# Up-projection of a ConvFFN: from the Strassen to the Winograd form of the 7-product scheme, with two early products on raw quarters for ten alternate pairs

## The chip, the cores and the metric

The kernel runs on one core of a Trainium2 chip. The metric is the device time of one execution in microseconds.

## The reference

One layer of a hybrid encoder in float32, for 640 rows (512 prompt frames and 8 streams of 16 frames), 2048 wide: a conditioned RMSNorm, an input projection, gated DeltaNet heads beside sliding-window attention, an output projection with a gated residual, and then the ConvFFN that the change touches:

```
h2 = rms_norm(x, norm2_w) * (1 + scale2) + shift2
u = h2 @ w_up                       # 640 x 2048 by 2048 x 11264 (gate | up)
u_ext = concatenate([ffn_prev, u], axis=1)
u_c = causal_dwconv(u_ext, ffn_conv_w) + ffn_conv_b      # width 3
gt, up = split(u_c, 2, axis=-1)
x = x + gate2 * ((silu(gt) * up) @ w_down)
```

The last two rows of `u_ext` of each stream are an output too.

## The kernel before, in words

Every float32 matrix is split into a high part, rounded to the matmul's float32r type, and the rest as a low part. A product is high x high, high x low and low x high, three matmuls for each 128 x 128 block of weights.

**Up-projection.** The 11264 columns of `w_up` are 88 blocks of 128, interleaved so that blocks 2i and 2i+1 are the gate and the up part of pair i; there are 44 pairs. For each pair the two blocks, the two halves of the 2048 inner columns, and the two halves `s` of the 640 rows (320 columns on chip) make a 2 x 2 by 2 x 2 product, done with 7 block products instead of 8. One block product is 8 inner chunks x 3 matmuls = 24 matmuls of 320 columns, in two weight units `h` of 128 x 512. For each unit: a weight sum `wsum` on VectorE, where the product wants one (5 of 7 products), a cast `whi` on ScalarE, the rest `wlo` on VectorE (`split_next`). `next_unit` keeps up to 4 units split, and weight sums are made 2 units ahead of that.

**Operands.** The activations' quarters are `b11, b12 = x[j]` (row halves 0 and 1 of chunk j) and `b21, b22 = x[j+8]`. `pipe` builds the background steps: multiply by the row's scale (`mul`, VectorE), modulate (`modulated`: ScalarE for the 256 prompt columns, GpSimd for the 64 others, tile `xr`), sum of quarters (`mixed`, on GpSimd, tile `st`), high part (`operand`, ScalarE), low part (`low`, VectorE). High and low parts lie in the tiles of the output projection's input (`mh`, `ml`), in `ex` and in the residual's own tiles (`op`). `feed` takes such steps from the list at a rate of so many per weight unit.

**Order.** Tiles are scheduled by hand: the program order is that of the Python code, and each engine works in order. In `attn_out` the output projection ends with eight blocks done first for row half 0 and then for row half 1, so that the norm and the operands of half 0 are made meanwhile. Then come the early products: products 2 and 4 of pairs 0 to 4, then 5 and 1 of the same pairs, combined on VectorE and GpSimd (`qsq`) and stored in the DRAM tile `pd`. In `ffn` those 5 pairs do only 3 products (6, 7, 3), and load what is stored through SP's queue (`t5`, `e` and a quarter of `fext`). The other 39 pairs do all seven in `ORDER`. The results of the seven products are summed into `fext` (the two blocks' rows before the convolution): on VectorE where PSUM is read, and on GpSimd for `e` and two `fext` quarters. The convolution of a pair (`conv`: `head` on ScalarE, four `tap` on VectorE, `silu`, `gatep`, `gated`, `store`) is cut into steps which run during the next pair, at half-product slots given by `SLOTS`, or `SLOTS2` when the next pair is a short one. The down-projection follows; it already uses the form of the scheme that the change brings to the up-projection.

Of the kernel before, what the change touches and what calls it, by code (L numbers as in the profile page):

```python
# [16 lines left out]
ORDER = (2, 4, 5, 1, 6, 7, 3)  # L17
# [4 lines left out]
NP = 5  # L22
# [7 lines left out]
MIXP = {4: (1, 1), 1: (1, 1), 6: (1, 1), 7: (1, 1), 3: (1, 1)}  # L30
SPOOL = {2: (1, 1), 5: (0, 0), 1: (1, 0), 6: (1, 1), 7: (0, 0)}
OPER = {5: ((0, 0), (0, 1), ALU.add), 2: ((1, 0), (1, 1), ALU.add), 1: ((0, 0), (1, 1), ALU.add), 3: ((0, 0),),
        7: ((0, 1), (1, 1), ALU.subtract), 6: ((1, 0), (0, 0), ALU.subtract), 4: ((1, 1),)}
SLOTS = (1, 3, 2, 4, 4, 6, 7, 8, 10, 10)
SLOTS2 = (9, 10, 9, 10, 10, 10, 11, 11, 11, 11)
# [193 lines left out]
class Kern:  # L229
# [81 lines left out]
    def build_stream(self):  # L311
        d = self.d
        self.units, self.upos, self.spos, self.apos, self.rpos = [], 0, 0, 0, 0
        self.rorder, self.rleft, self.rtile, self.utile, self.ltile = [], {}, {}, {}, {}
        for g in range(4):
            for i in range(3):
                self.add_unit(0, (("e", i, g), d["win"][i, :, g // 2, (g % 2) * 512:(g % 2 + 1) * 512]))
        for i in range(3, 44):
            self.add_block(("in", i), d["win"][i])
        for f in range(KC):  # L320
            self.add_block(("o", f), d["wo"][f])
        for f in range(KC - NF, KC):
            self.add_block(("O", f), d["wo"][f])

        def quarters(tag, i, ps, pool):
            for p in ps:
                for h in range(2):
                    o = OPER[p]
                    src = [((tag + "b" * (p == 3 and i < NP), 2 * i + j, r), d["wup"][2 * i + j][:, r]) for j, r in o[:2]]
                    self.add_unit(h, *src, op=o[2] if len(o) > 2 else None, pool=pool and len(o) > 2 and SPOOL[p][h])  # L330

        for ps in (ORDER[:2], ORDER[2:4]):
            for i in range(NP):
                quarters("v" + str(ps[0]), i, ps, True)
        for i in range(NFF):
            quarters("u", i, ORDER[4:] if i < NP else ORDER, i < NP)
        n = DGRP[0][1]
        for u in range(16 * n // 4):
            self.add_unit(u % 2, (("d", u // 2), d["wdn"][u // 2]))
        for job, p in self.djobs():  # L340
            f = 2 * n + 2 * job
            a = [[(("d", f + j), d["wdn"][f + j], r) for r in range(2)] for j in range(2)]
            t = {k: (("s", f, k), None, 0) for k in (5, 6)}
            src, op = {1: ((a[0][0],), None), 5: ((a[1][0], a[1][1]), ALU.add), 6: ((t.get(5), a[0][0]), ALU.subtract),
                       2: ((a[0][1],), None), 7: ((a[0][0], a[1][0]), ALU.subtract),
                       3: ((a[0][1], t.get(6)), ALU.subtract), 4: ((a[1][1],), None)}[p]
            self.add_unit(tuple(x[2] for x in src), *(x[:2] for x in src), op=op, pool=DPOOL.get(p),
                          keep=t[p][0] if p in t else None)
# [1205 lines left out]
    def phase2(self):  # L1554
# [6 lines left out]
        self.pd = tc.dram_tile([NP, 4, P, HALF], F32, name="pd")  # L1561
# [30 lines left out]
    def attn_out(self, pa, load):  # L1592
# [23 lines left out]
        self.ops, self.ex, self.low, self.temp, self.bg, self.due = {p: [] for p in ORDER}, [], {}, {}, [], 0.0  # L1616
# [11 lines left out]
        for part in range(2):  # L1628
            self.rate = RATE[1 + part]
            for n in range(NP):  # L1630
                t = [pa.tile([P, HALF], F32, tag=f"{x}{part}", name=f"q{x}") for x in ("acc", "sq")]
                if part:
                    m2 = pa.tile([P, HALF], F32, tag=("acc0", "sq0")[n % 2], name="qm2")
                    nc.sync.dma_start(out=m2, in_=self.pd[n, 0])
                for k in range(2):
                    ps = self.product(ORDER[2 * part + k])
                    if k == 0:
                        nc.scalar.copy(out=t[0], in_=ps)
                    else:
                        v.tensor_tensor(out=t[1], in0=ps, in1=t[0], op=(ALU.add, ALU.subtract)[part])  # L1640
                        if part:
                            nc.gpsimd.tensor_tensor(out=t[1], in0=t[1], in1=m2, op=ALU.subtract)
                    nc.sync.dma_start(out=self.pd[n, 2 * part + k], in_=t[k])
            if part == 0:
                self.drain("b")
# [13 lines left out]
    def modulated(self, k, s):  # L1659
# [8 lines left out]
        nc.gpsimd.tensor_tensor(out=xd, in0=xd, in1=bc(A), op=ALU.mult)  # L1668
        nc.gpsimd.tensor_tensor(out=xd, in0=xd, in1=bc(sh), op=ALU.add)

    def mixed(self, p, j):
        (b11, b12), (b21, b22) = self.x[j], self.x[j + 8]
        if p in (2, 5):
            return
        a, b, op = {4: (b21, b11, ALU.subtract), 1: (b11, b22, ALU.add), 6: (b11, b12, ALU.add),
                    7: (b21, b22, ALU.add), 3: (b12, b22, ALU.subtract)}[p]
        t = self.temp[p, j] = self.stile()
        e = self.nc.gpsimd if MIXP[p][j % 2] else self.nc.vector
        e.tensor_tensor(out=t, in0=a, in1=b, op=op)

    def operand(self, p, j):
# [3 lines left out]
        if p in (2, 5):  # L1685
            src = b11 if p == 2 else b22
        else:
            src = self.temp.pop((p, j))
        if p in (2, 4, 5, 1):
            c = HALF * (p in (5, 1))  # L1690
            hi, lo = (t[:, c:c + HALF] for t in self.mix[j + 8 * (p in (4, 1))])
        else:
# [3 lines left out]
            if p == 6:  # L1696
                self.ex.append(self.ox.tile([P, NT], F32R, tag=f"ex{j}", name=f"ex{j}"))
            lo = old(j + 8 if p == 7 else j, int(p == 3))
            hi = old(j + 8, 1) if p == 3 else self.ex[j][:, HALF * (p == 7):HALF * (p == 7) + HALF]
# [31 lines left out]
    def norm_half(self, pool, s, acc, rB):  # L1731
# [19 lines left out]
        if s == 0:  # L1751
            self.bg += self.pipe([[j, j + 8] for j in r], [[(2, j), (4, j)] for j in r], s, rB)
        else:
            self.bg += self.pipe([[j + 8] for j in r] + [[j] for j in r], [[(p, j)] for p in ORDER[2:] for j in r], s, rB)

    def next_bank(self):
        n = self.nbank % 4
        self.nbank += 1
        if n < 2:
            self.btile = [None, None] if n == 0 else self.btile  # L1760
            self.btile[n] = self.main_ps2(n)[0]
        return self.btile[n % 2][:, n // 2, 0:HALF]
# [20 lines left out]
    def ffn(self, fp):  # L1783
# [18 lines left out]
        def up(i):  # L1802
# [8 lines left out]
            e = hs[i] if i < NP else fp.tile([P, HALF], F32, tag="e", name="e")  # L1811
            for q, pr in enumerate(ORDER):
                if i < NP and q < 4:
                    continue
                ps = self.product(pr, lambda: mid(2 * q, t5))
                if pr == 2:
                    nc.scalar.copy(out=t2, in_=ps)
                elif pr == 4:
                    p4 = ps
                elif pr == 5:  # L1820
                    nc.scalar.copy(out=t5, in_=ps)
                    nc.gpsimd.tensor_tensor(out=e, in0=t2, in1=t5, op=ALU.add)
                elif pr == 1:
                    v.tensor_tensor(out=e, in0=ps, in1=e, op=ALU.subtract)
                    step(7)
                    ext = [prep(i, n) for n in range(2)]
                    add(v, quad(ext[1], 0), qin(p4), qin(t2))
                elif pr == 6:
                    v.tensor_tensor(out=t2, in0=ps, in1=e, op=ALU.add)
                elif pr == 7:  # L1830
                    v.tensor_tensor(out=e, in0=ps, in1=e, op=ALU.add)
                    if i < NP:
                        ext = list(short)
                    add(nc.gpsimd, quad(ext[0], 0), quad(ext[1], 0), qin(e))
                elif pr == 3:
                    add(v, quad(ext[0], 1), qin(ps), qin(t5))
                    add(nc.gpsimd, quad(ext[1], 1), quad(ext[0], 1), qin(t2))
                step(2 * q + 1)
                if i == NFF - 1 and q == 3:
                    self.lanes["c"].add(first_chunks())  # L1840
            conv(i, ext)

        short, hs = [], []

        def load_h():
            hs.append(fp.tile([P, HALF], F32, tag="e", name="e"))
            nc.sync.dma_start(out=hs[-1], in_=self.pd[len(hs) - 1, 3])

        def mid(slot, t5):
            step(slot)  # L1850
            n = self.pair
            if n < NP:
                if slot == 8:
                    nc.sync.dma_start(out=t5, in_=self.pd[n, 2])
                elif slot == 10:
                    short[:] = [prep(n, k) for k in range(2)]
                    for o, x in zip(quad(short[1], 0), qin(self.pd[n, 1])):
                        nc.sync.dma_start(out=o, in_=x)
                elif n < NP - 1:
                    load_h()  # L1860

        load_h()
# [13 lines left out]
        def conv(i, ext):  # L1876
# [38 lines left out]
            self.steps += sorted(zip(SLOTS2 if i + 1 < NP else SLOTS, fns), key=lambda x: x[0])  # L1915
# [289 lines left out]
```

## Time and profile before

| | |
|---|---|
| time, median of 3 runs | 3060.53 us (3060.45 to 3063.92) |
| profiled execution | 3059.98 us, span 3058.2 us |
| mean granted TensorE clock | 0.985 of full |
| TensorE (PE) busy | 2930.0 us, 96% |
| VectorE (DVE) busy | 2292.9 us, 75% |
| ScalarE (ACT) / GpSimd (POOL) busy | 1225.1 us, 40% / 842.0 us, 28% |

The output projection of the attention part ends at about 1342 us of the span, the early products at about 1456 us, the short pairs at about 1527 us, and the up-projection at about 2497 us. All instructions are recorded under one helper line (L91), so groups are told apart by tile names; the profile leaves out digits in names, so that `mm` and `mmd` are the two PSUM pools.

### The profile page before, as it was taken

The numbers are of one execution on the slowest core, as the hardware profiler recorded it, in microseconds if no ns is written. First come the engines' busy times: TensorE is split into PE (matmuls) and PEld (weight loads), VectorE is DVE, ScalarE is ACT, GpSimd is POOL, SyncE is SP. The second block draws the span as 40 slices with busy tenths as digits, with TensorE's granted clock in tenths as the row PEclk, the third lists the DMA queues.
The fourth block names the chain that finished last, engine by engine and source line by source line (L and its number), as shares of the span: only waits on it lengthen the run. The fifth ranks groups of instructions, "written<-read, shape, count | busy, mean of one in ns | idle before, by whom it ended". The sixth has DMA issues, their size and how long they took to land.

```text
span 3058.2 us, 53007 instructions
## 1 busy us (share of the span) xinstructions
PE 2930.0 (96%) x19649; PEld 2761.8 (90%) x19649; DVE 2292.9 (75%) x4419; ACT 1225.1 (40%) x2255; POOL 842.0 (28%) x1283
## 2 busy tenths in 40 slices
PE   5999999999999999987799999999999999999999
PEld 2688889998999987886799999999999999999998
DVE  4333446778887533589799989999899978999998
ACT  2323334333333322354344444444444454444432
POOL 2110012323233321167433333333333311111112
PEclk9999999999999999999999999999999999999999
DMA  8755542222223488745633333333333356666665
GB/s 341 288 177 181 185 130 83 79 77 72 83 90 115 161 300 295 235 141 189 200 99 98 98 101 102 103 98 99 107 104 98 98 180 217 204 226 207 213 221 191
DMA packets 219235, 480.74 MB, mean 157 GB/s; under 512 B 52082, under 2 KB 87184, under 8 KB 218960
## 3 DMA queue, kind: packets, MB, share of 16 engines
q1 hardware_dynamic: 185056, 429.99, 42.1%
q0 software_dynamic: 11152, 36.11, 3.5%
q10 hardware_dynamic: 22768, 11.25, 1.4%
q8 instruction: 155, 2.54, 0.3%
q14 instruction: 104, 0.85, 0.1%
HBM read 407.92 MB, written 71.18 MB: 157 GB/s over the span
## 4 chain that ended last, share of the span: by engine, by line
PE 75%; DVE 13%; DMA 5%; issue 4%; POOL 2%; ACT 1%; SPq 0%; DVEq 0%; ACTq 0%; POOLq 0%
PE mm L91 44%; PE mmd L91 20%; DVE wlo L91 4%; PE ada_ps L91 3%; DVE y L91 2%; PE inv_ps L91 2%; DVE wsum L91 1%; DVE dop L91 1%; DMA y<-yd 1%; DMA araw<-in_adaw 1%; PE pos L91 1%; DMA fext<-pd 1%; PE pstep L91 1%; PE pk L91 1%; DMA e<-pd 1%
## 5 line engine op out<-in xcount | busy, mean ns | idle before, releaser
L91 DVE TENSOR_TENSOR wlo<-raw,whi 128x512 fp32r<-128x512 f32 x584 | 445.1, 767 | 306.5 <-ACT whi L91 279.4
L91 ACT CAST whi<-raw 128x512 fp32r<-128x512 f32 x584 | 358.6, 619 | 498.0 <-PE mm L91 366.4
L91 ACT CAST whi<-wsum 128x512 fp32r<-128x512 f32 x600 | 367.2, 619 | 420.2 <-PE mmd L91 157.2
L91 DVE TENSOR_TENSOR wlo<-wsum,whi 128x512 fp32r<-128x512 f32 x600 | 423.2, 706 | 18.5 <-ACT whi L91 15.8
L91 DVE TENSOR_TENSOR wsum<-raw 128x512 f32<-128x512 f32 x455 | 344.9, 758 | 79.2 <-DMA raw<-in_wup 75.2
L91 PE MATMUL mm<-mh,wlo 128*128 128x320 f32 x1280 | 373.8, 312 | 10.1 <-DVE wlo L91 10.0
L91 PE MATMUL mm<-mh,whi 128*128 128x320 f32 x1280 | 373.3, 312 | 8.8 <-DVE qsq L91 6.5
L91 PE MATMUL mm<-ml,whi 128*128 128x320 f32 x1280 | 372.5, 311 | 0.0
L91 PE MATMUL mm<-hh,wlo 128*128 128x320 f32 x1376 | 331.4, 322 | 5.9 <-DVE wlo L91 5.9
L91 PE MATMUL mm<-hh,whi 128*128 128x320 f32 x1376 | 328.8, 320 | 4.5 <-ACT hh L91 3.2
L91 PE MATMUL mm<-hl,whi 128*128 128x320 f32 x1376 | 327.6, 320 | 0.0
L91 PE MATMUL mmd<-dop,whi 128*128 128x320 f32 x1280 | 283.8, 310 | 5.0 <-DVE y L91 4.9
L91 PEld LDWEIGHTS mm<-mh,wlo 128*128 128x128 f32 x1280 | 235.0, 189 | 23.9 <-DVE wlo L91 12.1
L91 PEld LDWEIGHTS mm<-mh,whi 128*128 128x128 f32 x1280 | 235.1, 189 | 19.6 <-ACT whi L91 7.2
L91 PEld LDWEIGHTS mm<-hh,whi 128*128 128x128 f32 x1376 | 231.0, 191 | 21.6 <-issue 13.7
L91 PEld LDWEIGHTS mm<-hh,wlo 128*128 128x128 f32 x1376 | 231.3, 191 | 19.8 <-issue 11.6
L91 PEld LDWEIGHTS mm<-hl,whi 128*128 128x128 f32 x1376 | 230.9, 191 | 19.2 <-issue 15.7
L91 PEld LDWEIGHTS mm<-ml,whi 128*128 128x128 f32 x1280 | 235.1, 189 | 6.9 <-issue 6.7
L91 PE MATMUL mmd<-mh,wlo 128*128 128x320 f32 x768 | 234.5, 312 | 6.1 <-DVE wlo L91 6.1
L91 PE MATMUL mmd<-mh,whi 128*128 128x320 f32 x768 | 234.6, 312 | 0.8 <-ACT qacc L91 0.8
L91 PE MATMUL mmd<-ml,whi 128*128 128x320 f32 x768 | 234.1, 312 | 0.4 <-DVE ml L91 0.4
L91 PEld LDWEIGHTS mmd<-dop,whi 128*128 128x128 f32 x1280 | 213.5, 188 | 7.7 <-ACT whi L91 4.8
(418 smaller groups left out, 6399.2 us busy)
## 6 DMA issues: line engine op xcount, KB each, us to landing
raw<-in_wup SPq DMA_DIRECT2D x206, 512.0 KB, 3.7
araw<-in_adaw SPq DMA_DIRECT2D x256, 256.0 KB, 5.1
raw<-in_wdn SPq DMA_DIRECT2D x88, 512.0 KB, 4.9
raw<-in_win SPq DMA_DIRECT2D x82, 512.0 KB, 3.6
araw<-in_adaw SPq DMA_DIRECT2D x64, 512.0 KB, 6.5
yd<-y SPq DMA_DIRECT2D x80, 320.0 KB, 5.0
y<-yd SPq DMA_DIRECT2D x80, 320.0 KB, 6.2
raw<-in_wo SPq DMA_DIRECT2D x48, 512.0 KB, 5.5
```

The source lines that it names most:

```text
L91: return f(*args, **kw)
```

## The change

The up-projection goes to the Winograd form, which has 4 weight sums and 4 operand sums. Weight sums per pair: product 5 uses a21+a22, product 6 that sum less a11, product 3 a12 less the sum of 6, product 7 a11-a21; products 1, 4 and 2 use raw quarters (`sum_unit`, shared now with the down-projection). A pair has 8 weight sums in place of 10. Operand sums: b12-b11, b22 less that, b22-b12 and b21 less the sum of the second, all on VectorE; products 1, 2 and 3 use raw quarters. Products 6, 3 and 7 accumulate in PSUM on the banks of 1, 5 and 4. Ten pairs (0, 2, ... 18) have products 1 and 2 done early, both in one bank, so that P1 and P1+P2 are copied to `pd`; such a pair then does five products. Their loads from `pd` are issued on GpSimd's queue. The sums of a pair are all on VectorE, and so are the 64-column operations of `modulated`.

```diff
-ORDER = (2, 4, 5, 1, 6, 7, 3)
+UPORD = (1, 5, 6, 4, 3, 7, 2)
-NP = 5
+NP = 10
+SHORT = {2 * k: k for k in range(NP)}
-SLOTS2 = (9, 10, 9, 10, 10, 10, 11, 11, 11, 11)
+SLOTS2 = (4, 6, 5, 7, 7, 8, 9, 10, 11, 11)
...
+        for i, p in self.first_jobs():
+            for h in range(2):
+                product("v", 2 * i, p, h)
+        for i in range(NFF):
+            for p in UPORD[1:6] if i in SHORT else UPORD:
                 for h in range(2):
+                    product("u", i, p, h)
...
+    def sum_unit(self, key, a, p, h, pool=False):
+        t = {k: (key + (k,), None, 0) for k in (5, 6)}
+        a = [[x + (i,) for x, i in zip(row, h)] for row in a]
+        src, op = {1: ((a[0][0],), None), 5: ((a[1][0], a[1][1]), ALU.add), 6: ((t[5], a[0][0]), ALU.subtract),
+                   2: ((a[0][1],), None), 7: ((a[0][0], a[1][0]), ALU.subtract),
+                   3: ((a[0][1], t[6]), ALU.subtract), 4: ((a[1][1],), None)}[p]
...
+    def first_jobs(self):
+        return [x[1:] for x in sorted((2 * i + 3 * (p - 1), i, p) for i in range(NP) for p in (1, 2))]
...
-        for part in range(2):
-            self.rate = RATE[1 + part]
-            for n in range(NP):
...
+        self.rate, banks = RATE[1], {}
+        for k, (n, p) in enumerate(self.first_jobs()):
+            if p == 1:
+                banks[n] = self.next_bank()
+            ps = self.product(p, None, 2, banks[n], p == 1)
+            t = pa.tile([P, HALF], F32, tag=("acc0", "sq0")[k % 2], name="part")
+            nc.scalar.copy(out=t, in_=ps)
+            nc.sync.dma_start(out=self.pd[n, p - 1], in_=t)
+        self.drain("b")
...
-        nc.gpsimd.tensor_tensor(out=xd, in0=xd, in1=bc(A), op=ALU.mult)
-        nc.gpsimd.tensor_tensor(out=xd, in0=xd, in1=bc(sh), op=ALU.add)
+        nc.vector.tensor_tensor(out=xd, in0=xd, in1=bc(A), op=ALU.mult)
+        nc.vector.tensor_tensor(out=xd, in0=xd, in1=bc(sh), op=ALU.add)
...
+        if p in (5, 7, 4):
+            a, b = {5: (b12, b11), 7: (b22, b12), 4: (b21, b11)}[p]
+            t = self.temp[p, j] = self.stile()
+            v.tensor_tensor(out=t, in0=a, in1=b, op=ALU.subtract)
+            if p == 5:
+                v.tensor_tensor(out=b11, in0=b22, in1=t, op=ALU.subtract)
...
+            self.bg += self.pipe([[j, j + 8] for j in r], [[(1, j), (2, j)] for j in r], s, rB)
...
+            self.bg += self.pipe([[j + 8] for j in r] + [[j] for j in r], [[(p, j)] for p in (3, 5, 7, 6, 4) for j in r], s, rB)
...
+            if short:
+                nc.gpsimd.dma_start(out=t2, in_=self.pd[SHORT[i], 0])
+            a, b, c = (self.main_ps2(self.nbank + k)[0] for k in range(3))
+            self.nbank += 3
+            bank = {1: a[:, 0], 6: a[:, 0], 5: b[:, 0], 3: b[:, 0], 2: b[:, 1], 4: c[:, 0], 7: c[:, 0]}
+            u2 = t2 if short else e
...
+                if pr == 1:
                     nc.scalar.copy(out=t2, in_=ps)
                 elif pr == 5:
                     nc.scalar.copy(out=t5, in_=ps)
+                elif pr == 6 and short:
+                    v.tensor_tensor(out=t2, in0=ps, in1=t2, op=ALU.add)
+                elif pr == 6:
+                    nc.scalar.copy(out=e, in_=ps)
+                elif pr == 4:
+                    v.tensor_tensor(out=t5, in0=t5, in1=ps, op=ALU.subtract)
+                elif pr == 3:
+                    step(9)
                     ext = [prep(i, n) for n in range(2)]
+                    add(v, quad(ext[0], 1), qin(ps), qin(u2))
+                    if short:
+                        for o, x in zip(quad(ext[0], 0), qin(self.pd[SHORT[i], 1])):
+                            nc.gpsimd.dma_start(out=o, in_=x)
                 elif pr == 7:
+                    add(v, quad(ext[1], 0), qin(ps), qin(u2))
+                    add(v, quad(ext[1], 1), quad(ext[1], 0), qin(t5))
+                elif pr == 2:
+                    add(v, quad(ext[0], 0), qin(ps), qin(t2))
```

## Rows read from the trace of the kernel before

**Rows 1.** The page: span, busy time, and VectorE in 40 slices.

```profile
span 3058.2 us, 53007 instructions
...
PE 2930.0 (96%) x19649; PEld 2761.8 (90%) x19649; DVE 2292.9 (75%) x4419; ACT 1225.1 (40%) x2255; POOL 842.0 (28%) x1283
...
DVE  4333446778887533589799989999899978999998
```

**Rows 2.** Busy time by stage: stretch, length, engines, clock, DMA share, GB/s.

```profile
1310.00:1341.65 31.65, 25.82 (x169) 24.73 (x167) 28.72 (x43) 17.73 (x39) 23.00 (x34) 0.99 0.38 121
1341.65:1526.97 185.32, 145.51 (x864) 136.54 (x863) 157.32 (x223) 79.20 (x151) 111.31 (x149) 0.92 0.58 187
1526.97:1545.30 18.33, 18.12 (x122) 17.85 (x123) 18.19 (x30) 9.02 (x17) 8.00 (x13) 1.00 0.27 84
1545.30:2497.00 951.70, 951.70 (x6491) 951.70 (x6491) 859.78 (x1428) 442.23 (x735) 317.60 (x521) 1.00 0.32 103
```

The engines stand in the order PE, PEld, DVE, ACT, POOL.

**Rows 3.** The chain of waits in order of time: start, us, what.

```profile
1312.97 1.14 POOL xr L91 x2
...
1384.04 1.09 DVE ml L91
...
1478.20 4.73 DMA fext<-pd
...
1484.69 4.63 DMA e<-pd
...
1494.05 5.04 DMA fext<-pd
...
1545.29 3.52 PE mmd L91 x24
```

**Rows 4.** Timeline of PE: first early product, first product of pair 5.

```profile
1341.65 0.47 PE L91 MATMUL mmd<-mh,whi 128*128 128x320 f32 x1
...
1526.97 0.39 PE L91 MATMUL mm<-mh,whi 128*128 128x320 f32 x1 [0.29 <-DVE e L91]
```

**Rows 5.** Groups of VectorE by shape, 1650 to 2350 us (full pairs).

```profile
L91 DVE TENSOR_TENSOR wsum<-raw 128x512 f32<-128x512 f32 x286 | 215.0, 752 | 58.9 <-DMA raw<-in_wup 55.9
L91 DVE TENSOR_TENSOR wlo<-wsum,whi 128x512 fp32r<-128x512 f32 x284 | 193.8, 682 | 9.0 <-ACT whi L91 7.8
...
L91 DVE SCALAR_TENSOR_TENSOR ftm<-fext,fcw,ftm 128x656 f32<-128x656 f32 x113 | 99.3, 899 | 0.0
...
L91 DVE TENSOR_TENSOR e<-mm,e 128x320 f32<-128x320 f32 x28 | 13.4, 477 | 0.0
...
L91 DVE TENSOR_TENSOR fext<-mm,t 128x256 f32<-128x256 f32 x29 | 12.0, 413 | 0.0
...
L91 DVE TENSOR_TENSOR fext<-mm,t 128x64 f32<-128x64 f32 x29 | 6.1, 211 | 0.0
```

**Rows 6.** Groups of VectorE and of GpSimd by shape, 1290 to 1460 us.

```profile
L91 DVE TENSOR_TENSOR wlo<-wsum,whi 128x512 fp32r<-128x512 f32 x34 | 35.8, 1054 | 3.6 <-ACT whi L91 2.8 <-POOL xr L91 0.7
...
L91 POOL TENSOR_TENSOR st<-xr,xr 128x320 f32<-128x320 f32 x40 | 47.0, 1191 | 0.0
...
L91 POOL TENSOR_TENSOR xr<-xr,A 128x64 f32<-128x64 f32 x32 | 17.6, 551 | 10.5 <-DVE xr L91 10.3
```

**Rows 7.** Timeline of VectorE at the end of the output projection.

```profile
1335.06 4.07 DVE L91 TENSOR_TENSOR acc<-acc,sq 128x320 f32<-128x320 f32 x1 [1.03 <-ACT sq L91]
1339.05 0.68 DVE L91 TENSOR_TENSOR wlo<-raw,whi 128x512 fp32r<-128x512 f32 x1
1339.66 0.68 DVE L91 TENSOR_TENSOR wlo<-wsum,whi 128x512 fp32r<-128x512 f32 x1
1340.26 0.48 DVE L91 TENSOR_TENSOR ml<-xr,mh 128x320 fp32r<-128x320 f32 x1
1340.66 0.48 DVE L91 TENSOR_TENSOR ml<-st,mh 128x320 fp32r<-128x320 f32 x1
```

**Rows 8.** Tile `xd`: its stores on GpSimd's queue, 1250 to 1345 us.

```profile
DMA to landing us min/median/max: 2.1/2.2/3.9
```

More of the change, by code (lines that the diff above doesn't have):

```diff
@@ L323, in build_stream, with product @@
             self.add_block(("O", f), d["wo"][f])
-        def quarters(tag, i, ps, pool):
-            for p in ps:
-                for h in range(2):
[L328 to L336, printed above, removed]
+        def product(tag, i, p, h):
+            a = [[((tag, 2 * i + j, r), d["wup"][2 * i + j][:, r]) for r in range(2)] for j in range(2)]
+            self.sum_unit(("s", tag, i, h), a, p, (h, h))
+        for i, p in self.first_jobs():
[3 more added lines that the diff above has]
+            for p in UPORD[1:6] if i in SHORT else UPORD:
+                for h in range(2):
+                    product("u", i, p, h)
         n = DGRP[0][1]
@@ L341, in build_stream @@
             f = 2 * n + 2 * job
[L342 to L348, printed above, removed]
+            a = [[(("d", f + j), d["wdn"][f + j]) for r in range(2)] for j in range(2)]
+            self.sum_unit(("s", "d", job), a, p, (0, 1), DPOOL.get(p))
+    def sum_unit(self, key, a, p, h, pool=False):
[4 more added lines that the diff above has]
+                   3: ((a[0][1], t[6]), ALU.subtract), 4: ((a[1][1],), None)}[p]
+        self.add_unit(tuple(x[2] for x in src), *(x[:2] for x in src), op=op, pool=pool,
+                      keep=t[p][0] if p in t else None)
+    def first_jobs(self):
+        return [x[1:] for x in sorted((2 * i + 3 * (p - 1), i, p) for i in range(NP) for p in (1, 2))]
     def djobs(self):
@@ L1615, in attn_out @@
                 done(f, i, ps[:, i, 0:HALF])
-        self.ops, self.ex, self.low, self.temp, self.bg, self.due = {p: [] for p in ORDER}, [], {}, {}, [], 0.0
+        self.ops, self.ex, self.low, self.temp, self.bg, self.due = {p: [] for p in UPORD}, [], {}, {}, [], 0.0
         for i in range(2):
@@ L1627, in attn_out @@
         self.drain("w")
-        for part in range(2):
-            self.rate = RATE[1 + part]
-            for n in range(NP):
[L1631 to L1645, printed above, removed]
+        self.rate, banks = RATE[1], {}
[7 more added lines that the diff above has]
+        self.drain("b")
         self.feed(99)
@@ L1667, in modulated @@
         xd = x[:, 256:HALF].rearrange("p (b t) -> p b t", t=TS)
-        nc.gpsimd.tensor_tensor(out=xd, in0=xd, in1=bc(A), op=ALU.mult)
-        nc.gpsimd.tensor_tensor(out=xd, in0=xd, in1=bc(sh), op=ALU.add)
+        nc.vector.tensor_tensor(out=xd, in0=xd, in1=bc(A), op=ALU.mult)
+        nc.vector.tensor_tensor(out=xd, in0=xd, in1=bc(sh), op=ALU.add)
     def mixed(self, p, j):
+        v = self.nc.vector
         (b11, b12), (b21, b22) = self.x[j], self.x[j + 8]
[L1673 to L1679, printed above, removed]
+        if p in (5, 7, 4):
[4 more added lines that the diff above has]
+                v.tensor_tensor(out=b11, in0=b22, in1=t, op=ALU.subtract)
     def operand(self, p, j):
@@ L1684, in operand @@
         (b11, b12), (b21, b22) = self.x[j], self.x[j + 8]
[L1685 to L1691, printed above, removed]
+        src = self.temp.pop((p, j)) if p in (5, 7, 4) else {1: b11, 2: b21, 3: b22, 6: b11}[p]
+        if p in (1, 2, 3, 5):
+            c = HALF * (p in (3, 5))
+            hi, lo = (t[:, c:c + HALF] for t in self.mix[j + 8 * (p in (2, 3))])
         else:
@@ L1751, in norm_half @@
         if s == 0:
[L1752 removed]
+            self.bg += self.pipe([[j, j + 8] for j in r], [[(1, j), (2, j)] for j in r], s, rB)
         else:
[L1754 removed]
+            self.bg += self.pipe([[j + 8] for j in r] + [[j] for j in r], [[(p, j)] for p in (3, 5, 7, 6, 4) for j in r], s, rB)
     def next_bank(self):
[L1757 removed]
         self.nbank += 1
[L1759 to L1762, printed above, removed]
+        return self.main_ps2(self.nbank)[0][:, 0, 0:HALF]
     def product(self, p, step=None, nh=2, ps=None, first=True):
@@ L1810, in up @@
             t2, t5 = (fp.tile([P, HALF], F32, tag=n, name=n) for n in ("t2", "t5"))
-            e = hs[i] if i < NP else fp.tile([P, HALF], F32, tag="e", name="e")
-            for q, pr in enumerate(ORDER):
-                if i < NP and q < 4:
+            e = None if i in SHORT else fp.tile([P, HALF], F32, tag="e", name="e")
+            short = i in SHORT
+            if short:
+                nc.gpsimd.dma_start(out=t2, in_=self.pd[SHORT[i], 0])
+            a, b, c = (self.main_ps2(self.nbank + k)[0] for k in range(3))
@@ L1814, in up @@
+            self.nbank += 3
+            bank = {1: a[:, 0], 6: a[:, 0], 5: b[:, 0], 3: b[:, 0], 2: b[:, 1], 4: c[:, 0], 7: c[:, 0]}
+            u2 = t2 if short else e
+            ext = []
+            for q, pr in enumerate(UPORD):
+                if short and pr in (1, 2):
                     continue
-                ps = self.product(pr, lambda: mid(2 * q, t5))
-                if pr == 2:
+                ps = self.product(pr, lambda: step(2 * q), 2, bank[pr][:, 0:HALF],
+                                  pr in (1, 5, 4, 2) or short and pr == 6)
+                if pr == 1:
@@ L1817, in up @@
                     nc.scalar.copy(out=t2, in_=ps)
-                elif pr == 4:
-                    p4 = ps
                 elif pr == 5:
                     nc.scalar.copy(out=t5, in_=ps)
[L1822 to L1825, printed above, removed]
+                elif pr == 6 and short:
[6 more added lines that the diff above has]
+                    step(9)
@@ L1826, in up @@
                     ext = [prep(i, n) for n in range(2)]
-                    add(v, quad(ext[1], 0), qin(p4), qin(t2))
-                elif pr == 6:
-                    v.tensor_tensor(out=t2, in0=ps, in1=e, op=ALU.add)
+                    add(v, quad(ext[0], 1), qin(ps), qin(u2))
+                    if short:
+                        for o, x in zip(quad(ext[0], 0), qin(self.pd[SHORT[i], 1])):
+                            nc.gpsimd.dma_start(out=o, in_=x)
                 elif pr == 7:
[L1831 to L1837, printed above, removed]
+                    add(v, quad(ext[1], 0), qin(ps), qin(u2))
@@ L1838, in up @@
+                    add(v, quad(ext[1], 1), quad(ext[1], 0), qin(t5))
+                elif pr == 2:
+                    add(v, quad(ext[0], 0), qin(ps), qin(t2))
                 step(2 * q + 1)
-                if i == NFF - 1 and q == 3:
+                if i == NFF - 1 and q == 2:
                     self.lanes["c"].add(first_chunks())
             conv(i, ext)
[L1843 to L1862, printed above, removed]
@@ L1914, in conv @@
                    lambda: tap(0, 2), silu, gatep, gated, store)
-            self.steps += sorted(zip(SLOTS2 if i + 1 < NP else SLOTS, fns), key=lambda x: x[0])
+            self.steps += sorted(zip(SLOTS2 if i + 1 in SHORT else SLOTS, fns), key=lambda x: x[0])
         ap = self.ap
```

12 lines of the change are left out of this document (4 added, 8 removed).

## Prediction

> **What bounds the kernel now.** I read the page first. TensorE (PE) is busy 96% of the span and VectorE (DVE) 75%, but the slices of DVE show that it is no average: it is at 9 or more tenths in the second half [rows 1]. So the question is which stage leaves PE waiting, and I cut the second half with the busy time by stage. The pairs 5 to 43, from 1545.3 to 2497 us, have PE busy for all of 951.7 us and at full clock, with DVE at 859.8 [rows 2]: there PE is the bound, a product of 24 matmuls takes 3.52 us [rows 3], a full pair 7 x 3.52 = 24.64, and no saving on DVE or GpSimd (POOL) can show. The change does not alter the number of products: 20 are taken early before and after (four for 5 pairs, now two for 10), and the rest later. What can change is PE's lost time, and it lies in one place.
>
> That place has three parts. (a) The end of the output projection, 1310 to 1341.65 us: 169 matmuls, which at 3.52/24 = 0.1467 us are 24.8 us, in 31.65 us: 6.9 lost [rows 2, 3]. (b) and (c) From the first early product to the first product of pair 5 [rows 4]: 185.32 us for 20 early products and 5 short pairs of 3, 35 x 3.52 = 123.2: 62.1 lost, of which 39.8 are idle PE (185.32 - 145.51) and most of the rest goes with a granted clock of 0.92, that is, some of it at the lower level of 1.2 GHz [rows 2]. (d) To 1545.3, five products in 18.33: 0.7. Together 69.7 us, and that is nearly all there is to win.
>
> The chain of waits names the causes. At the end of the projection it runs through POOL's small multiplies on the residual (`xr`) and its sums `st`; in the early products through DVE's splits and `ml`; in the short pairs through two loads from `pd` one after the other, `fext<-pd` and then `e<-pd`, of about 5 us each, and comes round every 15.9 us, where three products are 10.56 [rows 3]. The first two causes are one: DVE and POOL hinder each other. Alone, DVE starts a 512-column split 0.60 us after the one before and a 320-column sum after 0.40 [rows 7]; in this stretch the same split averages 1.05, and one 320-column `acc` sum takes 4.07 [rows 6, 7]. POOL's 320-column sums take 1.19 us [rows 6].
>
> **The change, part by part.**
>
> *Output projection and first operands.* The 64 `xr` operations on 64 columns (0.55 us each on POOL [rows 6]) go to DVE, where 64 columns cost 0.21 by the row and 0.14 after pipelining [rows 5]. No operand sum is left in the first half (products 1 and 2 take raw quarters), so POOL keeps one small residual add per block. The background feeds 0.4 steps per weight unit of 1.76 us, one step per 4.4 us. DVE needs per step two multiplies and two low parts (4 x 0.40), four small operations (0.14 to 0.21, 0.8 at most), 2.5 splits (1.5), and its share of residual and `acc` work (two rows of `fext` size and a 0.40 sum per 4 units: about 0.55): 4.45 at the most. It hardly fits. What POOL lost disappears, but DVE is full: of 6.9 us I leave 3 (0 if the small operations pipeline, 7 if nothing is won).
>
> *Early products.* All 20 need only operands 1 and 2, ready from the first half, so PE need not wait for the second norm; it is hidden behind 70.4 us of products. Before, two of four products needed operands of the second half. DVE's work in these 40 units: 40 splits x 0.60 = 24; the second half's 16 multiplies x 0.40 = 6.4; 32 small x 0.14 to 0.21 = 4.5 to 6.7; mixed operands 5 (two sums), 7 and 4, 32 x 0.40 = 12.8; 40 low parts x 0.40 = 16; the short chain of the norm, about 4 (the same as now); first sums 1.8. Sum 70 to 72 us against PE's 70.4. The weight sums of before and the `qsq` sums are gone; products 1 and 2 accumulate in one bank, and each needs only a ScalarE (ACT) copy and a store. So DVE is exactly full, and it is front-loaded: at 1.3 steps per unit the first 16 steps (multiply, two small, low, and from the eleventh on two mixed) put some 28 us on DVE in 12 units of 1.76 = 21.6 us. Up to three split units lie ahead, 5.3 us. I take 7 us lost, 0 if the lead covers it, 18 if the splits stay at 1.05 us [rows 6] for want of the relief.
>
> *Entry into the pairs.* The tiles of this stage hand their space to the tiles of the pairs; the first `t2` load waits for that. It is needed 7 us after the pair begins. 3 us, 0 to 8.
>
> *Short pairs.* Ten of them, at 0, 2, ... 18, with five products (17.6 us), between full pairs (24.64). DVE per full pair is now 859.78/951.7 x 24.64 = 22.26 us [rows 2]. After: two weight sums fewer (0.752 less 0.07 of overlap, 2 x 0.68), two 320-column sums fewer (2 x 0.41) and two two-piece adds more (2 x (0.34 + 0.14)) [rows 5]: 22.26 - 1.36 - 0.82 + 0.96 = 21.04. A short pair has four splits (4 x 0.61) and one two-piece add (0.48) fewer and one 320-column sum more: 18.53, at prices which still hold POOL's hindrance. So a short pair asks 0.9 us more of DVE than PE takes, the full one beside it 3.6 less; the two together 39.6 against 42.24, and the lead in split units lends the difference. DVE's waits for raw weights (58.9 us in 700 [rows 5], about 2 per pair) are of an engine that is ahead. I take 0.3 us per short pair, 3 in all; 0 to 16 (1.6 us each, if nothing is lent and prices are the means of the rows).
>
> *Loads of the early products.* `t2<-pd` and `ext[0]<-pd` go from SP's queue to POOL's. The `t2` load waits until the pair before has added its last product, and is used after product 6, 7.04 us into the pair. Stores from POOL's queue landed in 2.1 to 3.9 us with DVE some 90% busy [rows 2, 8]. Queued behind it on POOL are only `fext` clears and state copies, which are needed ten microseconds later. The `ext[0]` load is issued after product 3 and is first read after product 5 of the next pair, some 10 us on. Nothing, with 3 us of cover. The ten fewer 512-KB weight loads lie beside PE and give nothing.
>
> *New waits in a pair.* Products 6, 3 and 7 accumulate on the banks of 1, 5 and 4, whose readers have at least one product (3.52 us) of time; the one on DVE, `t5 - ps`, is due as soon as product 4 ends, where DVE waits anyway. Nothing. In full pairs POOL's chain of `e` and `fext` sums, up to now hidden behind PE, goes away: nothing either.
>
> *Clock.* The remaining 16 us of stalls will cost some low clock: now 39.8 us idle go with 0.08 x 185 = 15 us of it, so 6; and the small matmuls of the norm stay, 1.5.
>
> **Sum.** Lost after: 3 + 7 + 3 + 3 + 6 + 1.5 = 23.5 us against 69.7: 46 us won. The profiled execution took 3059.98 us, 1.8 over its span and 0.55 under the median: 3059.98 - 46 = 3014, with the median's half microsecond and roundings 3014 still. I forecast 3014 us.
>
> **A rule against it.** Stores that POOL issues land within 3.9 us while DVE runs at 90% [rows 2, 8]. The Trainium skill (SBUF — State Buffer, SBUF: two separate sides) warns that a DMA issued from the GpSimd queue can starve, since the engine is shut out of the port that it shares with VectorE and can't write descriptors, and advises the SP or ACT queue; that would make the loads late. The page ties this to VectorE's two-port modes, which it says two-input sums do not have; no run so far shows such a delay for loads from `pd`. This is rival 2.
>
> **Rivals.**
> 1. *The early stage stays DVE-bound, or the alternation does.* For it: DVE at 100% of PE's time in my own sum. Against: POOL's hindrance goes. With splits at 1.05 us, 11 us more than I took; with 1.6 us per short pair, 13 more: with either 3025 to 3027, with both 3038. Chance 0.22.
> 2. *The loads on POOL's queue become the wait of every short pair*, as `fext<-pd` and `e<-pd` are now. The place is `t2` after product 6. PE stalls when the load lands later than 7.04 + 5.3 (the split units ahead) = 12.3 us into the pair; the change is slower than before when each of the ten loses more than (46 + 6)/10 = 5.2 us, a landing after 17.5 us. At 7 us each the time is 3014 + 70 = 3084. Against: landings of 2.1 to 3.9 us [rows 8]. Chance 0.05.
> 3. *It does not free PE*: the lost time is set by the second norm's chain wherever it stands, and the ten short pairs lose in all what the five did (25 us) and the early products what they did: 3060. Chance 0.02; the chain needs operands that the first 20 products no longer use.
> 4. *All slack is used*: 5 us lost in all, 3059.98 - 64.7 = 2995. Chance 0.05.
> The forecast itself (2997 to 3024): 0.66.
>
> **Numbers.** About 0.2% (6 us) is what a measurement here can tell from no change. Faster: 0.66 + 0.22 + 0.05 = 0.93; same 0.02; slower 0.05. The range 2997 to 3037 holds the forecast's cases and most of rival 1's.
>
> **What would show it.** Right: POOL's `st` and `xr` groups gone, and its busy time in the full pairs down by about half; 20 early products in under 85 us; a pair of short and full in 42.3 us with PE at 100%; full pairs from 20 on unchanged at 24.64; the chain of waits all PE from the first short pair on. Wrong: DVE at 100% with PE below 90% over the early products longer than 85 us; PE waiting for `wlo` in each short pair; DVE waiting for `t2<-pd`; PE waiting for `t5` before product 7.

## The result, and the profile after

The changed kernel takes 3008.94 us (median of 4 runs, 3005.06 to 3011.95) against 3060.49; the ratio is 0.9831, 95% interval 0.9814 to 0.9848. The forecast was 3014 us, in a range of 2997 to 3037. The same kernel run again with the last experiments gave 3009.55.

The page of the kernel after: span, busy time, VectorE (DVE) in 40 slices.

```profile
span 3006.0 us, 52752 instructions
...
PE 2916.6 (97%) x19649; PEld 2748.6 (91%) x19649; DVE 2191.2 (73%) x4535; ACT 1237.7 (41%) x2299; POOL 556.8 (19%) x964
...
DVE  4233345778788442479888888888888869999998
```

Busy time by stage (columns as in [rows 2]): the end of the output projection, the early products in three pieces up to 1414 us, a stretch with short pairs (a full pair between each two), one of full pairs alone; and below, in one line, the whole stage of the twenty early products.

```profile
1310.00:1338.26 28.26, 27.32 (x184) 26.60 (x182) 24.21 (x65) 19.45 (x42) 3.46 (x8) 1.00 0.43 141
1338.26:1360.00 21.74, 21.73 (x154) 20.63 (x153) 16.09 (x47) 12.74 (x28) 0.87 (x2) 1.00 0.58 201
1360.00:1391.00 31.00, 26.50 (x162) 24.92 (x161) 30.31 (x83) 20.75 (x45) 0.00 (x0) 0.94 0.37 128
1391.00:1414.00 23.00, 23.00 (x158) 23.00 (x158) 21.74 (x47) 18.34 (x44) 0.00 (x0) 1.00 0.66 225
...
1420.00:1650.00 230.00, 230.00 (x1570) 230.00 (x1569) 201.29 (x370) 109.37 (x183) 42.32 (x108) 1.00 0.39 127
...
1850.00:2400.00 550.00, 550.00 (x3752) 550.00 (x3752) 454.09 (x826) 261.58 (x449) 89.35 (x190) 1.00 0.31 100
```

```profile
1338.26:1419.70 81.44, 76.92 (x509) 74.25 (x508) 73.84 (x184) 55.16 (x121) 0.87 (x2) 0.98 0.51 175
```

One stall is left, at 1360 to 1391 us, with DVE busy 30.3 of 31 us. From there on the TensorE (PE) is busy to 1650 us without a gap, through more than half of the short pairs, and idle for 0.1 us in the rest of them. The early products and short pairs of before took 185 us for 123 [rows 2, 4]. The chain of waits of the kernel after says the same; a few pieces of it:

```profile
1366.21 0.55 DVE xr L88 x2
1366.93 0.48 DVE ml L88
1367.41 0.60 DVE wlo L88
...
1390.99 7.05 PE mmd L88 x48
1398.05 7.04 PE mm L88 x48
```

**One measure for all kernels.** Single runs of one kernel differ by 5 us and more, partly in stages that no edit touches (PE had 8257 instructions behind it at 1300 us before, 8242 after). So I count PE's instructions from 1300 to 2400 us of the span, where every kernel is somewhere between the output projection and the last full pairs: 1100 us less 3.52/24 = 0.1467 us for each is the time lost there. (The small matmuls of the norm count like the others, and a few records are missing; the changed kernel, run twice, gave 7440 and 7441, and experiments 5 and 8, which cost nothing in this stretch, 7441 each.) Kernel before, then after:

```profile
1300.00:2400.00 1100.00, 1054.15 (x7047) 1043.82 (x7046) 984.59 (x1591) 509.81 (x879) 439.51 (x679) 0.99 0.36 116
```

```profile
1300.00:2400.00 1100.00, 1094.45 (x7440) 1090.79 (x7439) 937.68 (x1788) 548.57 (x967) 176.31 (x404) 1.00 0.36 117
```

1100 - 7047 x 3.52/24 = 66.4 us lost before, 8.8 after: 57.6 us won here. The spans differ by 52.2. The other 5 went outside: by the same count the changed kernel is 2 us behind at 1300 us, and loses 24 us after 2400 us where the kernel before lost 21. Whether the change has a part in that is not shown; experiment 1, in the old scheme, loses 24 there too.

A correction to what stands above: the first short pair before begins at 1444.3 us, where `ex` first feeds PE, not at 1456. So of the 62.1 us, 32 were lost in the early products (102.6 us for 70.4) and 30 in the short pairs (82.7 for 52.8):

```profile
1341.65:1444.28 102.63, 84.29 (x503) 78.70 (x503) 97.21 (x132) 48.84 (x100) 72.59 (x78) 0.92 0.51 169
1444.28:1526.97 82.69, 61.22 (x363) 57.84 (x361) 60.10 (x92) 30.36 (x51) 38.71 (x72) 0.92 0.67 209
```

### The profile page after: what moved, and what is told of

The parts are those of the page before. It is cut to its first block, busy times and chain, and to the rows that moved or that the text cites. A ratio compares the mean times of both kernels' runs of the same rounds, so it can differ in the third digit from the quotient of the medians.

```text
span 3006.0 us, 52752 instructions
## 1 busy us (share of the span) xinstructions
PE 2916.6 (97%) x19649; PEld 2748.6 (91%) x19649; DVE 2191.2 (73%) x4535; ACT 1237.7 (41%) x2299; POOL 556.8 (19%) x964
## 4 chain that ended last, share of the span: by engine, by line
PE 72%; DVE 12%; issue 10%; DMA 3%; POOL 2%; ACT 1%; SPq 0%; ACTq 0%; DVEq 0%; POOLq 0%
PE mm L88 40%; PE mmd L88 22%; DVE wlo L88 3%; PE ada_ps L88 2%; DVE y L88 2%; PE inv_ps L88 2%; DVE wsum L88 1%; DVE dop L88 1%; DMA araw<-in_adaw 1%; POOL xr L88 1%; PE pos L88 1%; PE pstep L88 1%; POOL xd L88 1%; PE pk L88 1%; PE pl L88 0%
## 5 line engine op out<-in xcount | busy, mean ns | idle before, releaser
L88 DVE TENSOR_TENSOR wlo<-raw,whi 128x512 fp32r<-128x512 f32 x672 | 481.2, 721 | 338.2 <-ACT whi L88 310.2
L88 ACT CAST whi<-raw 128x512 fp32r<-128x512 f32 x672 | 413.3, 619 | 500.5 <-PE mm L88 359.9
L88 ACT CAST whi<-wsum 128x512 fp32r<-128x512 f32 x512 | 317.1, 619 | 391.9 <-PE mmd L88 170.5
L88 DVE TENSOR_TENSOR wlo<-wsum,whi 128x512 fp32r<-128x512 f32 x512 | 349.7, 688 | 92.3 <-ACT whi L88 91.2
L88 PE MATMUL mm<-dop,whi 128*128 128x320 f32 x960 | 213.1, 310 | 4.2 <-DVE y L88 3.9
```

Source lines behind the costliest of these rows:

```text
L88: return f(*args, **kw)
```

## The experiments

My theory was that DVE and GpSimd (POOL) hinder each other, that twenty products on raw quarters hide the second half's preparation, and that alternation with fewer loads frees the short pairs. The main rival: the place of the sums does not matter, only the scheme does.

### 1. The sums of the kernel before on VectorE

```diff
-MIXP = {4: (1, 1), 1: (1, 1), 6: (1, 1), 7: (1, 1), 3: (1, 1)}
-SPOOL = {2: (1, 1), 5: (0, 0), 1: (1, 0), 6: (1, 1), 7: (0, 0)}
+MIXP = {4: (0, 0), 1: (0, 0), 6: (0, 0), 7: (0, 0), 3: (0, 0)}
+SPOOL = {2: (0, 0), 5: (0, 0), 1: (0, 0), 6: (0, 0), 7: (0, 0)}
...
-        nc.gpsimd.tensor_tensor(out=xd, in0=xd, in1=bc(A), op=ALU.mult)
-        nc.gpsimd.tensor_tensor(out=xd, in0=xd, in1=bc(sh), op=ALU.add)
+        nc.vector.tensor_tensor(out=xd, in0=xd, in1=bc(A), op=ALU.mult)
+        nc.vector.tensor_tensor(out=xd, in0=xd, in1=bc(sh), op=ALU.add)
...
-                            nc.gpsimd.tensor_tensor(out=t[1], in0=t[1], in1=m2, op=ALU.subtract)
+                            v.tensor_tensor(out=t[1], in0=t[1], in1=m2, op=ALU.subtract)
```

> The kernel before, its scheme and its five short pairs kept, with the operand sums, the early pairs' weight sums, the sums of the early products and the 64-column operations moved from GpSimd to VectorE. My theory (the two engines hinder each other, but the early stage has also too much VectorE work in this scheme): the early products' stage shortens from 114 us to about 96 to 102, which is VectorE's own sum for it, the output projection's end loses 3 us less, the short pairs stay at 15.4 to 15.9 us each because their loads set them: 3040 to 3052 us. Rival (GpSimd carried work off VectorE, which is the bound there): the 114 us of GpSimd work come on top of a full VectorE, 3085 us or more.

Measured: 3046.54 us, ratio 0.9959 (0.9944 to 0.9974); 7154 instructions and 50.7 us lost from 1300 to 2400 us (the stretch of every such count below). The early products, then the short pairs:

```profile
1338.97:1437.00 98.03, 85.17 (x540) 79.97 (x538) 94.16 (x223) 51.47 (x107) 1.24 (x2) 0.97 0.60 196
1437.00:1510.42 73.42, 58.26 (x326) 55.31 (x325) 54.84 (x95) 27.23 (x44) 22.25 (x56) 0.86 0.67 212
```

VectorE's list of the early stage, by shape:

```profile
L91 DVE TENSOR_TENSOR wlo<-wsum,whi 128x512 fp32r<-128x512 f32 x36 | 24.8, 688 | 1.6 <-ACT whi L91 1.6
L91 DVE TENSOR_TENSOR wsum<-raw 128x512 f32<-128x512 f32 x36 | 24.7, 686 | 0.0
L91 DVE TENSOR_TENSOR st<-xr,xr 128x320 f32<-128x320 f32 x32 | 15.6, 487 | 0.0
```

A split takes 0.688 us where it took 1.054 [rows 6], so DVE does POOL's work as well, and the twenty products take a little less time, 98.0 us (before 102.6). The short pairs, which I had expected to stay as they were, lose 20.6 us instead of 30 (the weight sums of their product 6 have moved to DVE too); their chain of waits is still that of the loads:

```profile
1462.34 5.52 DMA fext<-pd
...
1469.58 3.27 DMA e<-pd
...
1494.11 4.98 DMA fext<-pd
```

So the hindrance is real, and ending it by this move is worth some 16 us net, less than a third of the gain: 9 in the short pairs, 5 in the early products, 2 at the end of the projection.

### 2. The changed kernel with operand sums and 64-column operations on GpSimd

```diff
-        nc.vector.tensor_tensor(out=xd, in0=xd, in1=bc(A), op=ALU.mult)
-        nc.vector.tensor_tensor(out=xd, in0=xd, in1=bc(sh), op=ALU.add)
+        nc.gpsimd.tensor_tensor(out=xd, in0=xd, in1=bc(A), op=ALU.mult)
+        nc.gpsimd.tensor_tensor(out=xd, in0=xd, in1=bc(sh), op=ALU.add)
...
     def mixed(self, p, j):
-        v = self.nc.vector
+        v = self.nc.gpsimd
```

> The changed kernel with the operand sums and the 64-column operations back on GpSimd. My theory (hindrance): the splits and low parts of the early products slow down again and the stage of 20 products grows from 76 us by 10 to 25, 3018 to 3035 us. Rival (the gain is in the raw operands of the first 20 products, wherever the sums run, since PE no longer waits for the second half): 3005 to 3013 us, as the changed kernel.

Measured: 3008.15 us (3007.05 to 3012.46); 7416 instructions, 12.3 us lost. My theory fell here: the hindrance comes back in the rows, but not in the time.

```profile
1300.00:2400.00 1100.00, 1092.38 (x7416) 1088.38 (x7416) 933.35 (x1692) 545.84 (x962) 235.66 (x491) 1.00 0.36 116
```

```profile
L88 DVE TENSOR_TENSOR wlo<-raw,whi 128x512 fp32r<-128x512 f32 x34 | 29.6, 872 | 11.4 <-ACT whi L88 11.4
...
L88 DVE TENSOR_TENSOR ml<-st,mh 128x320 fp32r<-128x320 f32 x8 | 8.3, 1039 | 1.3 <-ACT mh L88 1.3
```

Splits are slow again (0.872 us), yet only 3.5 us more are lost than in the changed kernel. What POOL takes off DVE about pays for what it costs, but not evenly: with the 64-column operations alone on POOL 4.1 us are lost (experiment 9), so the operand sums cost 8 us there and the small operations save nearly 5. POOL's operations on `xr` and `st` make 26% of the chain from 1340 to 1420 us, and ScalarE waits 14.5 us for the sums from 1340 to 1400; how much of the loss is that wait, and how much the slow splits, was not separated.

### 3. Consecutive short pairs

```diff
-SHORT = {2 * k: k for k in range(NP)}
+SHORT = {k: k for k in range(NP)}
```

> The changed kernel with pairs 0 to 9 as the short ones in place of 0, 2, ... 18. My theory: VectorE's 18.5 us at the prices of before, or some 17.1 at the clean prices of the changed trace, stand against 17.6 us of PE; with clean prices nothing is lost (3006 to 3012 us), with the others 0.9 us for each of ten (3018 us). Rival (a short pair needs a full one beside it, to hide its loads and the convolution before it): as in the kernel before, 3 to 5 us for each of ten, 3040 to 3060 us.

Measured: 3032.57 us (3027.83 to 3034.43); 7242 instructions, 37.8 us lost, 29 more than alternate. The time lies between the two expectations. The whole stretch, then the timelines of VectorE and of SP's queue in one pair:

```profile
1300.00:2400.00 1100.00, 1075.46 (x7242) 1067.74 (x7241) 913.66 (x1743) 532.69 (x939) 201.28 (x394) 0.99 0.36 114
```

```profile
1481.67 0.68 DVE L88 TENSOR_TENSOR wsum<-raw 128x512 f32<-128x512 f32 x1
1482.28 0.68 DVE L88 TENSOR_TENSOR wlo<-wsum,whi 128x512 fp32r<-128x512 f32 x1
1487.10 0.69 DVE L88 TENSOR_TENSOR wsum<-raw 128x512 f32<-128x512 f32 x1 [4.14 <-DMA raw<-in_wup]
```

```profile
1474.62 2.29 SPq L88 DMA_DIRECT2D md<-ftm  x2
1482.38 1.79 SPq L88 DMA_DIRECT2D raw<-in_wup  x4
```

DVE is not full; it stands 4.1 us a pair (eight times from 1420 to 1590 us) for a weight load issued at 1482.38, the moment that its sum of 1481.67, the last of product 7, has given back a raw tile. Neither of my two mechanisms, but a third.

### 4. Consecutive, with a22 loaded first

```diff
-        src, op = {1: ((a[0][0],), None), 5: ((a[1][0], a[1][1]), ALU.add), 6: ((t[5], a[0][0]), ALU.subtract),
+        src, op = {1: ((a[0][0],), None), 5: ((a[1][1], a[1][0]), ALU.add), 6: ((t[5], a[0][0]), ALU.subtract),
```

> The kernel of the consecutive short pairs, with one more edit: product 5 names its quarters as a22 + a21, so that a22 is loaded before a21. The five raw tiles are a ring; now a21's load takes the tile of the pair's first quarter, which is given back two products earlier. My theory (each short pair waits some 4 us for a weight load that could not be issued before product 7 of the pair before gave a tile back): the wait falls to about that of the next quarter, 1 to 2 us, and 12 to 22 of the 25 us come back: 3010 to 3020 us. Rival (the wait is for the early products' loads or the convolution's tiles on GpSimd's queue): no change, 3027 to 3037 us.

Measured: 3010.50 us (3006.50 to 3011.59); 7443 instructions, 8.4 us lost: all 29 us came back with one swapped pair of names.

```profile
1300.00:2400.00 1100.00, 1093.28 (x7443) 1089.62 (x7442) 939.05 (x1788) 547.56 (x967) 192.44 (x404) 1.00 0.36 117
```

So the order of loads in the ring of raw tiles, and nothing else, made consecutive short pairs dear. That in the alternate order a full pair's product 2 and the next one's product 1 give the loads the time is my reading; no run tests it.

### 5. Loads on SP's queue

```diff
-                nc.gpsimd.dma_start(out=t2, in_=self.pd[SHORT[i], 0])
+                nc.sync.dma_start(out=t2, in_=self.pd[SHORT[i], 0])
...
-                            nc.gpsimd.dma_start(out=o, in_=x)
+                            nc.sync.dma_start(out=o, in_=x)
```

> The changed kernel with the loads of the early products issued on SP's queue in place of GpSimd's. My theory: the load of t2 waits on SP for the last sum of the pair before, and the weight loads queue behind it; up to 2 us per short pair where the weights come late, 3009 to 3030 us. Rival (a load on GpSimd's queue is starved while VectorE works, so SP is the better place): faster than the changed kernel, below 3005 us; but PE is shown busy all through the short pairs there, so there is nothing to win.

Measured: 3001.20 us (3000.22 to 3003.68), below 3005 as the rival has it, but 7441 instructions, one more than the changed kernel: nothing is lost or won in the stage, so the lower time is not the loads' doing there. PE had 8262 instructions behind it at 1300 us, 20 more than in the changed kernel's profile, so some 3 us of the lower total arose ahead of the edit; where the rest of it came from stays open. In the changed kernel the loads on POOL's queue landed in 2.3 to 4.1 us, here on SP's in 2.2 to 6.2:

```profile
DMA to landing us min/median/max: 2.3/2.6/4.1
```

```profile
DMA to landing us min/median/max: 2.2/4.9/6.2
```

### 6. Alternation alone, in the scheme of before

```diff
+SH = {2 * k: k for k in range(NP)}
...
-                if i < NP and q < 4:
+                if i in SH and q < 4:
...
-                elif n < NP - 1:
-                    load_h()
+            if slot == 12 and n + 1 in SH:
+                load_h()
```

The other tests of `i < NP` and the places in `pd` follow in the same way.

> The kernel before with its five short pairs at 0, 2, 4, 6, 8 in place of 0 to 4, all else kept. Rival to be tested: alternation alone frees the short pairs of their loads, and their 30 us of lost time go, 3030 to 3040 us. My theory: a three-product pair has 10.56 us of PE against some 15 us of VectorE work and the same two loads, of which the full pair beside it can lend only part; 5 to 20 us are won, 3040 to 3055 us.

Measured: 3064.83 us (10 runs), ratio 1.0019 (1.0009 to 1.0028); 6992 instructions, 74.5 us lost. Neither expectation: alternation makes the old scheme slower, by 8 us in this count and 6 in the medians. Its chain of waits shows where:

```profile
1527.81 4.57 DMA raw<-in_wup
...
1534.24 1.74 POOL fext L92 x2
1536.00 5.64 DMA e<-pd
```

A weight load stands in the chain at four of the five short pairs, and the load of `e` behind it at three. `e` has one tile: its load starts when POOL's `fext` sums of the full pair have read it, and DVE's sum after product 6 waits for it. So the run tests alternation with this one tile; with more tiles for `e` it was not run.

### 7. Half as many early products

```diff
-NP = 10
+NP = 5
-RATE = (0.4, 1.3, 1.0)
+RATE = (0.4, 2.6, 1.0)
```

> The changed kernel with ten early products for five short pairs (0, 2, ... 8) in place of twenty, and the background steps fed at 2.6 per unit, so that they are again all given out within the stage. My theory: it is the number of early products on raw quarters that hides the second half's preparation: 10 products are 35 us, VectorE's work there is 60 to 65 us, so 20 to 30 us more are lost: 3027 to 3040 us. Rival (short pairs have a cost of their own, so fewer of them are as good): 3003 to 3014 us.

Measured: 3023.43 us (3018.14 to 3029.31); 7309 instructions, 28.0 us lost, 19 more than with ten pairs, all before 1410 us:

```profile
1350.00:1370.00 20.00, 13.99 (x91) 12.95 (x89) 18.78 (x58) 15.06 (x32) 0.00 (x0) 0.98 0.29 101
1370.00:1390.00 20.00, 15.32 (x59) 13.86 (x60) 19.53 (x49) 11.66 (x26) 0.00 (x0) 0.59 0.30 95
1390.00:1410.00 20.00, 15.58 (x79) 13.67 (x79) 20.00 (x44) 11.68 (x27) 8.52 (x9) 0.83 0.24 73
1410.00:1430.00 20.00, 20.00 (x138) 20.00 (x137) 13.99 (x26) 8.92 (x15) 2.54 (x5) 0.99 0.33 114
```

That is some 4 us under what I expected, but on the theory's side: DVE is 97% busy for 60 us, PE has products for 35 of them, and part of the stalled time passes at a granted clock of 0.59. The doubled rate of the steps belongs to the edit; what it costs by itself was not tested.

### 8. Ten weight sums in the full pairs

The two sums of product 7 are computed twice in pairs 20 to 43.

> The changed kernel with the two weight sums of product 7 computed twice in each of the pairs 20 to 43, so that VectorE makes ten weight sums per pair there again. My theory: full pairs are bound by PE, the saving of the 4+4 form is not seen there, and the 24 x 1.2 us of added work disappear under PE: 3004 to 3012 us, pairs at 24.64 us. Rival (VectorE's load counts in the full pairs too): up to 29 us longer, 3015 to 3038 us.

Measured: 3006.23 us; the full pairs:

```profile
1850.00:2400.00 550.00, 550.00 (x3752) 550.00 (x3751) 478.28 (x871) 257.63 (x446) 88.59 (x189) 1.00 0.31 101
```

DVE does 24 us more, PE the same 3752 matmuls: the two weight sums that the scheme saves are worth nothing in a full pair.

### 9. The steps spread, and the 64-column operations alone on GpSimd

```diff
+            self.rate = 0.9 if k < 12 else 1.75
```

> The changed kernel with the background steps of the second half fed at 0.9 per weight unit during the first 12 early products and at 1.75 after, in place of 1.3 throughout. My theory: the one stall that is left (31 us for 162 matmuls, 7 us lost) comes from VectorE's work being bunched where multiplies, modulation and two operand sums of product 5 fall together; spread out, it fits under PE, and 5 to 7 us of it go: 3000 to 3005 us. Rival (the second norm's chain or ScalarE sets the stall): no change, 3005 to 3012 us, with the stall moved.

Measured: 3005.88 us (3003.73 to 3007.01), 7438 instructions, 9.1 us lost. The idle time moved to 1370 to 1430 us (3.6 us of it) and the loss did not shrink; with this spread at least, bunching does not decide. Other spreads were not run.

> The changed kernel with the 64-column operations alone back on GpSimd, the operand sums on VectorE. My theory now (VectorE's own sum in the stage of the early products is as long as PE's, so what is taken off it shortens the stall): VectorE loses 6 us of work in the stage and GpSimd hinders it less than with the sums: 2 to 5 us faster than the changed kernel. Rival (any GpSimd work there costs VectorE as much as it saves): as the changed kernel, within 2 us.

> The changed kernel again, unedited, beside the others on the same chip, to have an interval for the few microseconds that tell its variants apart: 3003 to 3011 us.

Measured: 3004.57 us (3000.02 to 3008.64) with the two operations of `modulated` on GpSimd, 7472 instructions, 4.1 us lost; the changed kernel beside it 3009.55 (3004.21 to 3014.61) and 7441, 8.7 lost. Of the 4.6 us between them 2.5 lie in the stall at 1360 to 1391 us, which has 179 instructions where it had 162:

```profile
1360.00:1391.00 31.00, 27.31 (x179) 26.00 (x178) 30.52 (x65) 21.96 (x50) 6.64 (x14) 1.00 0.45 161
```

```profile
1300.00:2400.00 1100.00, 1096.20 (x7472) 1093.78 (x7470) 936.85 (x1740) 549.68 (x969) 204.52 (x466) 1.00 0.36 118
```

The intervals against the kernel before (0.9811 to 0.9845, and 0.9825 to 0.9864) overlap, so the totals alone don't tell the two apart; the stage does. Of all versions this one loses least in the stage; the lowest median is that of experiment 5 (3001.20), which the stage does not account for.

## Why the prediction was right, point by point

- *The number.* Nearer than the working deserves. In its stage the change won 57.6 us where 46 were forecast: the loss that is left, 8.8 us (12 as the sum counts it: 81.44 - 70.4 for the early products, and 1.3), lies nearer to the 5 of rival 4 than to the forecast's 23.5. Of the 11 or 12 us between, only 5 show in the time, because about as much went ahead of and behind the stage, for which the sum had no term. That part is luck.
- *Where the loss lay.* Right: 57.6 of the 66.4 us between 1300 and 2400 us went, and full pairs kept their 24.64 us; experiment 8 shows that DVE's saving does not count there.
- *Output projection's end.* 3 us forecast; 28.26 - 184 x 0.1467 = 1.3 measured. DVE was not full, as feared, but 86% busy (24.21 of 28.26 us). From 1310 to 1345 us POOL's `xr` operations were 34% of the chain before; the one small residual add per block that is left makes 3% of it.
- *Early products.* 7 us forecast at the front of the stage; (31 - 162 x 0.1467) = 7.2 measured, later than forecast (PE idle from 1370 to 1390 us, 30 us and more into the stage) but among the steps named, with DVE at 98% and its row of multiply, modulation and operand-5 sums in the chain. The sum "70 to 72 us against 70.4" was the right reading (73.84 us measured, in a stage of 81.44): spreading the work gains nothing (9), taking work off DVE gains 4.6 us (9), halving the products costs 19 (7). Bunching, which I gave as the reason for 7 rather than 0, is not borne out.
- *Hindrance of the two engines.* The step that I got wrong in kind. I called it the cause of the first two losses, 39 us; moving the sums off POOL is worth 6 us in those two parts of the old scheme and 9 in the short pairs, where I had not put it (1), and 3.5 in the new one (2). Where the rows showed slow instructions I took their price for the price of the stage.
- *Entry and short pairs.* 3 + 3 us forecast, none measured: PE is busy for all of 1420 to 1650 us. DVE's load over a short and a full pair was 201.29/230 x 42.24 = 37.0 us against the 39.6 of the sum; a weight sum fell from 0.753 to 0.687 us and a split of a raw block from 0.794 to 0.688 (means of 1550 to 2400 us before and 1440 to 1650 us after), which is about 2 of the 2.6 us. That alternation was needed is true with this order of loads, but not for the reason given (DVE's lent time): the raw ring decides (3, 4). What freed the short pairs of their 30 us is only narrowed down: not the order of the pairs (4, 6) and not the queue of the loads (5). The longer pair (17.6 us for 10.56) and the loads' new places in it were changed together, and no run separates them.
- *Loads on POOL's queue.* Costed at nothing, and nothing (5). The stores that I leaned on were issued over 1250 to 1345 us, where DVE was 69% busy (65.54 of 95 us); 90% held only from 1310 us on. The rule of the Trainium skill (SBUF — State Buffer, SBUF: two separate sides) on starved GpSimd-queue loads, which the page ties to VectorE's two-port modes, did not bite: the loads landed in 4.1 us at most, and on SP's queue they were no faster.
- *Clock.* 6 us forecast. The granted clock of the remaining stall is 0.94 over 31 us, so about 2, and inside the 7.2 above. This, the two empty terms and the projection's end are why the sum put some 11 us too much into the stage.
- *Rivals.* 1 came in kind but not at its price: the early stage is still bound by DVE at its one stall, for 7 us and not 18; in the pairs it did not come (DVE at 0.88 of PE's time there). 2 is excluded by the landings (5), 3 by the result. 4 came near in the stage (8.8 us lost for 5), not in the time.

## What to carry to other kernels

Before moving work between engines, ask what the waiting engine is short of: here, in the early products, ready operands more than the speed of the engine that makes them. Ten more products on raw data, done while the others' operands are prepared, were worth 19 us (7); moving the sums off POOL, 16 us in the old scheme (1) and 3.5 in the new one (2). Where the pattern of a loop changes, follow each ring of buffers through the new order, and look at who gives back the tile that the first load of the next round takes; with consecutive short pairs the order of the names in one sum was worth 29 us. When an edit is smaller than the spread of whole runs, count the bounding engine's instructions in the stage.

## What the runs showed of the hardware

A split of 512 columns on VectorE with both inputs in SBUF takes 0.69 us where GpSimd hardly works (1.24 of 98 us, experiment 1) and 0.87 on average where it runs sums beside it for 49 of 80 us (2). The Trainium skill (SBUF — State Buffer, Who interferes with whom) says that a VectorE instruction with two SBUF inputs contends with a GpSimd one that reads SBUF, through a read interface that they share; the rows agree in direction. I had not expected how little of this reached the time. Nor had I expected the clock: over 20 us the granted clock was 0.59, most of it at the lower level of 1.2 GHz, after PE had been idle for 6 of the 20 us before (7), while it stayed at 1.00 with 3.6 us idle in 60 (9).
